# Four kinds of small products taken off TensorE, and the instruction order of a hybrid attention, DeltaNet and expert layer planned anew

## The chip, the cores and the metric

The kernel runs on one core of a Trainium2 chip. The metric is the device time of one execution in microseconds (us), from its first to its last instruction with what lies around it. Each time below is such a time, or a stretch of the one execution that the profiler recorded.

## What is computed

Two layers work on 256 latent tokens and 256 context tokens of width 1024. Each layer has a token mixer and a mixture of sixteen experts; the second layer needs results for the latent tokens alone.

```
for l in range(2):
    m_lat, m_ctx = six rows each of silu(c) @ mod_w[l] + mod_b[l]     # shift, scale, gate; twice
    h = modulate(x, ...)                                              # both streams
    q, k, v, qkv, z, a, b, gates = split(h @ w_in[l])                 # one projection
    A: differential attention, 2-D rotary positions on the latent q and k
       rope: x1*cos - x2*sin, x2*cos + x1*sin
    B: qkv = silu(short_conv(qkv)); q, k scaled to unit length over 128 channels
       g = cumsum of log decays; decay[i, j] = exp(g[i] - g[j]) where i >= j
       a_mat = beta * (k k^T) * decay (strict); solve (I + a_mat) against values
       out = q state + (q k^T * decay) v_new; the state goes on from chunk to chunk, both directions
    x = layer_norm(alpha*x + gate * (sig(gA)*(A @ w_pa) + sig(gB)*(B @ w_pb)) @ w_o)
    router: 4 groups of 4 experts, the best group, in it the best 2
    x = layer_norm(alpha*x + gate * sum of w * (silu(h@w1[e]) * (h@w3[e])) @ w2[e])
```

## The kernel before

**Strands.** The kernel is written as some ninety generators ("strands"): `modulation`, `conv_worker`, `norms`, `build`, `double`, `scan`, `att_worker`, `expert_up` and so on, one or several per stage and layer. A strand yields a class of buffer (`page`: 128x2048 words, twenty of them; `t5`: 128x512, sixteen; `tiny`; `bank`: the eight PSUM banks) or an `Event`, and records operations through helpers (`mm`, `tr`, `tt`, `stt`, `cpy`, `dma`). Since helpers record, the profile's lines are theirs: L451 is `mm`, L463 `mm_beside`, L468 `tr` (transpose on TensorE against the identity), L489 `tt`, L518 `stt`, L485 `cpy` on ScalarE, L537 `dma`.

**Planner.** While the program is being built, `Scheduler.run` keeps a clock of its own. Each helper gives its operation a duration (`dve`, `acte`, `n / 2400` for a fast product). `plan` estimates when a strand's first operation could begin; among those that could begin within 0.05 us of the earliest, the one whose strand has the lowest number in `PRIO` is emitted. So estimated durations and `PRIO` fix the order in every engine's queue, and each queue then runs in that order, whatever the real times are. That holds for SP's queue too, on which the weight loads and most other transfers stand: a transfer emitted behind a load that waits for its page waits with it.

**Stages.** Weights are loaded in 1 MB pieces in the order of `PLAN` (`loader`), split into a high and a low part for three fast products (`splitter`, `mm3`), and multiplied. In layer 0 projections, convolutions, the inverse of the decay matrix and attention run interleaved; then come the gates, the output projection, and the router (a run of small VectorE operations). Fourteen of the sixteen experts' weights can be asked for only when the router has ranked them (`pos_ev`). Layer 1 repeats this.

**Places that the change touches.**
- `modulation`: products of `csil` with `mod_w` leave four partial sums on the partitions; for eight of a layer's twelve pieces `mm(bk[:2, :], K["sel2"], part, True, True)` adds them with one float32 product of 512 columns (two TensorE records).
- `conv_worker`: `mm(Y.sqs[...], a4[:, t, :], ones[:, 0:1], True, True)` sums squares over channels, one product per head and tile of 128 tokens, into one PSUM bank (`sqb`) that stays taken through the stage, until `sq_end`.
- `build` and `double` call `grow`, which makes rows of cumulated decays with four transposes of a column spread over 128 columns, into a bank; `stt` reads them from there.
- `double` computes, per (tile, direction), part of the inverse (its products are 32 and 64 rows high) and, behind a wait for the q convolution, the matrix P = q k^T * decay.
- `att_worker`: the rotary swap of 16-row halves is `mm(b.v(256), K["perm"], lat, True, True)`, then three `tt`.

Of the kernel before, what the change touches and what calls it, by code (L numbers as in the profile page):

```python
# [38 lines left out]
def slot0(l, q):  # L39
# [15 lines left out]
PRIO = {"0ab": 2.106, "0att": 5.949, "0atte": 5.963, "0attend0": 3.942, "0attend1": 2.095, "0attw0": 3.982, "0attw1":  # L55
# [16 lines left out]

def const_layout():
# [5 lines left out]
    blk["perm"] = (r == (c ^ 16))  # L79
# [17 lines left out]
    blk["selR"] = (q[:, None] == np.arange(16)[None, :])  # L97
    blk["neg16"] = np.where(q < 16, -1.0, 0.0)[:, None]
# [52 lines left out]
class Op:  # L151
    __slots__ = ("opts", "outs", "ins", "ready", "nbytes", "pen", "rows")

    def __init__(self, opts, outs, ins, nbytes=0, pen=0.0):
        self.opts, self.outs, self.ins, self.nbytes, self.pen = opts, outs, ins, nbytes, pen
        self.ready = None
        self.rows = ins[-1].shape[0] / 128 if opts[0][0] == "PE" else 0.0
# [11 lines left out]
class Scheduler:  # L169
# [4 lines left out]
    PE_IN, PE_OUT = 0.1, 0.06  # L174
    DGE = 0.45
    TICK, COLUMNS = 10.24 / 3, 3060

    def __init__(self, make):
# [8 lines left out]
        self.now = 0.0  # L187
        self.columns, self.floor = {}, {}
# [142 lines left out]
    def plan(self, op):  # L331
# [15 lines left out]
    def emit(self, op, o, st):  # L347
# [5 lines left out]
        if eng == "PE":  # L353
            k = int(st / self.TICK)
            self.columns[k] = self.columns.get(k, 0.0) + op.opts[0][1] * 2400 * op.rows
            end += self.PE_OUT
        if op.nbytes:
# [6 lines left out]
            end = x + max(op.nbytes / 410e3, 0.1)  # L364
# [41 lines left out]
def tile_kernel(ctx, tc, x_in, c_in, ctx_in, cctx_in, mod_w, mod_b, w_in, conv_w, lam_q1, lam_k1, lam_q2,  # L406
# [13 lines left out]
    inv_dram = [dp.tile([128, 256], F32, name=f"inv{i}_dram") for i in range(2)]  # L420

# [37 lines left out]
    def mm_beside(os, as_, bs, start, stop):  # L459
# [4 lines left out]
        SC.rec([("PE", width(bs[0]) / 600 + 0.008 * len(os), f)], list(os), [*as_, *bs])  # L464

    def tr(o, a, idn=None):
        idn = ident if idn is None else idn
        SC.rec([("PE", 0.11, lambda: PE.transpose(o, a, idn))], [o], [a])  # L468
# [14 lines left out]
    def cpy(o, a):  # L483

        SC.rec([("ACT", acte(width(o), in_psum(a)), lambda: S.activation(o, a, AF.Copy, bias=0.0, scale=1.0)),  # L485
                ("DVE", dve(width(o), in_psum(a), 0.5), lambda: V.tensor_copy(o, a))], [o], [a], pen=1.0)
# [6 lines left out]
    def neg(o, a):  # L493
        SC.rec([("ACT", acte(width(o), in_psum(a)), lambda: S.activation(o, a, AF.Copy, bias=0.0, scale=-1.0)),
                ("DVE", dve(width(o), in_psum(a), 0.5), lambda: V.tensor_scalar(o, a, -1.0, None, op0=OP.mult))],
# [6 lines left out]
    def ts(o, a, s1, op0, s2=None, op1=None):  # L502
# [4 lines left out]
        SC.rec([("DVE", dve(width(o), in_psum(a), 0.5), f)], [o], aps(a, s1, s2))  # L507

    def affine(o, a, s, b):

        SC.rec([("ACT", acte(width(o), in_psum(a)), lambda: S.activation(o, a, AF.Identity, bias=b, scale=s)),
                ("DVE", dve(width(o), in_psum(a), 0.5),
# [8 lines left out]
    def vcopy(o, a):  # L521
        SC.rec([("DVE", dve(width(o), in_psum(a), 0.5), lambda: V.tensor_copy(o, a))], [o], [a])
# [2048 lines left out]
```

## Time and profile before

| | us |
|---|---|
| median of 3 runs | 1632.36 (1616.32 to 1634.97) |
| the profiled execution | 1628.14 |
| its span | 1626.0 |
| TensorE busy in it | 1493.8 |
| VectorE busy | 931.7 |
| ScalarE busy | 535.8 |

The span is the stretch from the first to the last instruction; 2.14 us of the profiled execution lie around it. PE is TensorE's products, PEld its weight loads, DVE VectorE, ACT ScalarE, POOL GpSimd, SP the queue of the sync engine. "Busy" of PE is the time covered by products, whose ends are modelled. PEclk is the granted share of TensorE's full clock of 2.4 GHz; 0.5 is the lower level, 1.2 GHz.

### The profile page before, as it was taken

The numbers are of one execution on the slowest core, as the hardware profiler recorded it, in microseconds if no ns is written. First come the engines' busy times: TensorE is split into PE (matmuls) and PEld (weight loads), VectorE is DVE, ScalarE is ACT, GpSimd is POOL, SyncE is SP. The second block draws the span as 40 slices with busy tenths as digits, with TensorE's granted clock in tenths as the row PEclk, the third lists the DMA queues.
The fourth block names the chain that finished last, engine by engine and source line by source line (L and its number), as shares of the span: only waits on it lengthen the run. The fifth ranks groups of instructions, "written<-read, shape, count | busy, mean of one in ns | idle before, by whom it ended". The sixth has DMA issues, their size and how long they took to land. (4 is left out here: it accounts for less than half of the span.)

```text
span 1626.0 us, 24829 instructions
## 1 busy us (share of the span) xinstructions
PE 1493.8 (92%) x9551; PEld 1017.6 (63%) x9552; DVE 931.7 (57%) x2391; ACT 535.8 (33%) x950; POOL 63.1 (4%) x84
## 2 busy tenths in 40 slices
PE   5999999999999977999999899999999957999974
PEld 2776788756787843465564367788889844454421
DVE  1677945768437586365575966792778666210023
ACT  2533343434331121264553253343554302110110
POOL 1000000000000001111010000000000000000000
PEclk9999999999999997999998999996999977999988
DMA  9415522152336577799998743440055955899994
GB/s 312 158 53 175 160 57 80 50 210 91 117 130 249 190 302 283 277 422 403 417 383 326 260 151 109 156 102 5 28 182 176 312 218 214 304 421 421 420 408 203
DMA packets 147725, 363.17 MB, mean 223 GB/s; under 512 B 27932, under 2 KB 82284, under 8 KB 122256
## 3 DMA queue, kind: packets, MB, share of 16 engines
q1 hardware_dynamic: 139808, 342.91, 56.9%
q0 software_dynamic: 6512, 16.38, 3.0%
q10 hardware_dynamic: 1280, 2.23, 0.4%
q8 instruction: 77, 1.26, 0.3%
q14 instruction: 48, 0.39, 0.1%
HBM read 345.47 MB, written 21.56 MB: 226 GB/s over the span
## 5 line engine op out<-in xcount | busy, mean ns | idle before, releaser
L451 PE MATMUL bank<-page,page 128*128 128x512 f32 (+3 forms) x3776 | 733.7, 349 | 13.5 <-ACT page L485 6.5
L451 PEld LDWEIGHTS bank<-page,page 128*128 128x128 f32 (+2 forms) x3776 | 567.6, 189 | 126.1 <-issue 27.3
L489 DVE TENSOR_TENSOR page<-page,page 128x1024 fp32r<-128x1024 f32 (+3 forms) x219 | 250.8, 1164 | 96.9 <-ACT page L485 94.9
L485 ACT ACTIVATE page<-page 128x1024 fp32r<-128x1024 f32 (+1 forms) x196 | 200.3, 1046 | 122.8 <-PE bank L451 65.8
L463 PE MATMUL bank<-page,t 128*64 128x512 f32 (+2 forms) x736 | 208.9, 607 | 6.8 <-DMA page<-in_w_exp_dram 5.9
L485 ACT ACTIVATE t<-bank 128x512 f32<-128x512 f32 (+5 forms) x168 | 79.8, 480 | 306.7 <-PE bank L468 210.5
L489 DVE TENSOR_TENSOR t<-bank,t 128x512 f32<-128x512 f32 (+3 forms) x63 | 49.6, 792 | 188.0 <-PE bank L463 153.8
L485 ACT ACTIVATE page<-bank 128x512 f32<-128x512 f32 (+2 forms) x127 | 70.2, 557 | 222.1 <-PE bank L451 97.9
L463 PE MATMUL bank<-page,page 128*32 128x512 f32 (+2 forms) x512 | 136.0, 604 | 8.0 <-DMA page<-in_w_exp_dram 7.6
L463 PEld LDWEIGHTS bank<-page,t 128*64 128x64 f32 (+2 forms) x736 | 64.6, 147 | 103.4 <-issue 87.1
L451 PE MATMUL bank<-t,page 32*32 32x16 f32 (+4 forms) x1472 | 117.1, 244 | 2.1 <-DVE t L504 1.8
L451 PEld LDWEIGHTS bank<-t,page 128*128 128x128 f32 (+3 forms) x1472 | 104.9, 160 | 18.9 <-issue 11.3
L468 PE MATMUL bank<-cf,t 128*128 128x128 f32 (+2 forms) x468 | 79.1, 287 | 36.0 <-DVE t L489 25.9
L468 PEld LDWEIGHTS bank<-cf,t 128*128 128x128 f32 (+2 forms) x468 | 54.8, 144 | 70.6 <-DVE t L489 31.8
L463 PEld LDWEIGHTS bank<-page,page 128*32 128x32 f32 (+2 forms) x512 | 47.0, 144 | 81.2 <-issue 67.1
L451 PE MATMUL bank<-page,csil 128*32 128x512 f32 x384 | 68.0, 678 | 17.2 <-DMA page<-in_mod_w_dram 16.5
L451 PE MATMUL bank<-page,t 128*128 128x512 f32 (+2 forms) x392 | 81.4, 346 | 2.1 <-DVE page L489 1.1
L451 PEld LDWEIGHTS bank<-page,t 128*128 128x128 f32 (+1 forms) x392 | 56.0, 185 | 26.4 <-issue 9.2
L518 DVE SCALAR_TENSOR_TENSOR t<-bank,tiny,t 128x508 f32<-128x508 f32 (+3 forms) x96 | 66.5, 700 | 7.5 <-ACT t L480 6.4
L480 ACT ACTIVATE t<-bank,tiny 128x512 f32<-128x512 f32 (+1 forms) x72 | 44.6, 623 | 53.5 <-PE bank L451 27.8
L480 ACT ACTIVATE page<-page 128x512 f32<-128x512 f32 (+2 forms) x44 | 25.6, 588 | 84.1 <-DVE page L489 48.5
L468 PE MATMUL bank<-cf,page 128*128 128x128 f32 (+1 forms) x248 | 41.7, 305 | 9.9 <-DMA page<-h_dram,cd 8.4
(178 smaller groups left out, 1139.7 us busy)
## 6 DMA issues: line engine op xcount, KB each, us to landing
page<-in_w_exp_dram SPq DMA_DIRECT2D x192, 1024.0 KB
page<-in_mod_w_dram SPq DMA_DIRECT2D x48, 1024.0 KB
page<-in_w_in_dram SPq DMA_DIRECT2D x44, 1024.0 KB
page<-in_w_o_dram SPq DMA_DIRECT2D x8, 1024.0 KB
y_dram<-t POOLq DMA_DIRECT2D x6, 1024.0 KB, 8.3
page<-m_dram SPq DMA_DIRECT2D x12, 512.0 KB
page<-y_dram SPq DMA_DIRECT2D x6, 1024.0 KB
page<-in_w_pb_dram SPq DMA_DIRECT2D x4, 1024.0 KB
```

The costliest lines, as they stand in the source:

```text
L451: lambda: PE.matmul(o, a, b, start=start, stop=stop, skip_group_check=True))], [o], [a, b])
L463: PE.matmul(o, a, b, start=start, stop=stop, skip_group_check=True)
L468: SC.rec([("PE", 0.11, lambda: PE.transpose(o, a, idn))], [o], [a])
L480: SC.rec([("ACT", acte(width(o), in_psum(a)), lambda: S.activation(o, a, f, bias=bias, scale=scale, **k))], aps(o, accum_out), aps(a, bias ...
L485: SC.rec([("ACT", acte(width(o), in_psum(a)), lambda: S.activation(o, a, AF.Copy, bias=0.0, scale=1.0)), ("DVE", dve(width(o), in_psum(a), ...
L489: opts = [("DVE", dve(width(o), in_psum(a) or in_psum(b)), lambda: V.tensor_tensor(out=o, in0=a, in1=b, op=op)), ("POOL", 0.1 + width(o) * ...
L518: lambda: V.scalar_tensor_tensor(o, a, s, b, op0=op0, op1=op1, **k))],
```

## The change

- `grow` is gone. `decay_gates` writes the cumulated decays of a layer once to a DRAM tensor (`gc_dram`, 16 KB); `build` reads them back spread over all partitions with one 1 MB transfer per pair of tiles, on SP; `double` asks for the rows again per (tile, direction), 256 KB each, on SP (`sum_rows`).
- The part of `double` behind the inverse becomes strands of its own (`decayed`).
- Squares are summed by four products side by side (32 columns each, on `ones`), a copy, and one short product per tile; no bank stays taken.
- The partial sums of the modulation rows are split into a high and a low part and added by two fast products with 16 columns.
- The rotary swap is a VectorE shuffle into a `t5`.
- The planner's durations are other ones, a change of product shape is charged 0.09 us (`TURN`), a transfer on the ACT queue 0.45 us, and all of `PRIO` is new.

```diff
-PRIO = {"0ab": 2.106, "0att": 5.949, ...
+PRIO = {"0ab": 2.106, "0att": 5.949, ...
...
+    TURN = 0.09
...
+                if op.kind != self.kind:
+                    o = (o[0], o[1] + self.TURN, o[2])
...
-            end = x + max(op.nbytes / 410e3, 0.1)
+            end = x + max(op.nbytes / 420e3, 0.1)
...
+    gc_dram = [dp.tile([32, 128], F32, name=f"gc{l}_dram") for l in range(2)]
...
-        t = n / 2400 if b.dtype == BF or (b.dtype == F32R and n >= 256) else n / 600
+        t = n / 2250 if b.dtype == BF or (b.dtype == F32R and n >= 256) else n / 600
...
-            t = max(t, width(a) / 1200)
+            t = max(t, width(a) / 580)
...
     def dve(n, ps, r=1.0):
-        return 0.065 + n * 0.00104 * (1.0 if ps else r) + (0.06 if ps else 0.0)
+        return 0.15 + n * 0.00104 * (1.0 if ps else r) + (0.02 if ps else 0.0)
     def acte(n, ps):
-        return (0.05 if ps else 0.093) + n * 0.000834
+        return (0.175 if ps else 0.21) + n * 0.00082
...
-        SC.rec([(q, 1.0 if q == "POOL" else 0.45 if q == "SP" else 0.1, lambda: eng.dma_start(o, a))], [o], [a],
+        SC.rec([(q, 1.0 if q == "POOL" else 0.45, lambda: eng.dma_start(o, a))], [o], [a],
...
-            cpy(part, bk)
+            if kind < 2:
+                cpy(part, bk)
+            else:
+                lo_ = yield "t5"
+                split(pt_.r(512), lo_.r(512), bk)
...
-                mm(bk[:2, :], K["sel2"], part, True, True)
-                tt(part[:2, :], bk[:2, :], br, OP.add)
+                mm(bk[:16, :], sel2r, pt_.r(512), True, False)
+                mm(bk[:16, :], sel2r, lo_.r(512), False, True)
+                tt(br, bk[:2, :], br, OP.add)
...
-        Y.sqb = yield "bank"
-        Y.sqs = Y.sqb.v(2, 4, 4)
+        Y.sq = {}
...
-                for t in range(2 * ns):
-                    mm(Y.sqs[:, 1 - part, 2 * s0 + t, hd:hd + 1], a4[:, t, :], ones[:, 0:1], True, True)
+                Y.sq[part, hd] = a_
...
+        b = yield "bank"
+        n0 = 256 if Y.last and part == 0 else 0
+        mm_beside([b.v(512)[32 * hd:32 * hd + 32, n0:] for hd in range(4)], [ones[:, :32]] * 4,
+                  [Y.sq[part, hd].v(512)[:, n0:] for hd in range(4)], True, True)
+        st = yield "t5"
+        cpy(st.v(512)[:, n0:], b.v(512)[:, n0:])
...
+        for t in range(n0 // 128, 4):
+            mm(b.v(4, 16)[:, t], st.v(4, 128)[:, t], K["selH"], True, True)
...
+        tr(b.v(128)[:32], gv[:, 6, :])
+        cpy(rows_.v(128)[:32], b.v(128)[:32])
+        dma(dram(gc_dram[l], 0, [[128, 32], [1, 128]]), rows_.v(128)[:32])
...
-    def grow(Y, b, t, d):
-        for hd in range(4):
-            tr(b.v(4, 128)[:, hd, :], hcol(Y.GC, t, d, hd).to_broadcast([128, 128]))
-        return b.v(4, 128)
+    def sum_rows(Y, t, d):
+        dma(cell(Y.pA, t, d).rearrange("p h j -> p (h j)"),
+            dram(gc_dram[Y.l], (t * 8 + d * 4) * 128, [[0, 128], [1, 512]]))
...
+        if t % 2 == 0:
+            dma(Y.pA[si].v(2048), dram(gc_dram[Y.l], si * 2048, [[0, 128], [1, 2048]]))
+            SC.set(Y.gc_ev[si])
+        yield Y.gc_ev[si]
...
             if t in Y.tiles:
-                for hd in range(4):
-                    yield Y.conv_ev[0, hd]
-                b = yield "bank"
-                gr = grow(Y, b, t, d)
...
+                sum_rows(Y, t, d)
+            else:
+                SC.set(Y.p_ev[t, d])
+            SC.set(Y.u_ev[t, d])
+
+    def decayed(Y, groups):
+        for t, d in groups:
+            if t not in Y.tiles:
+                continue
+            yield Y.u_ev[t, d]
+            for hd in range(4):
+                yield Y.conv_ev[0, hd]
+            A = cell(Y.pA, t, d)
...
-                b = yield "bank"
-                mm(b.v(256), K["perm"], lat, True, True)
-                tt(tmp.v(256), b.v(256), K["sin"], OP.mult)
-                SC.free(b)
-                tt(lat, lat, K["cos"], OP.mult)
-                tt(lat, lat, tmp.v(256), OP.add)
+                SC.rec([("DVE", dve(256, False), lambda o=tmp.v(256), a=lat:
+                         V.stream_shuffle(out=o, in_=a, mask=[c ^ 16 for c in range(32)]))], [tmp.v(256)], [lat])
+                tt(tmp.v(256), tmp.v(256), K["sin"], OP.mult)
+                tt(tmp.v(256, o=256), lat, K["cos"], OP.mult)
+                tt(lat, tmp.v(256, o=256), tmp.v(256), OP.add)
```

## Rows read from the trace of the kernel before

**Rows 1.** The page: busy us of each engine (share of the span), instructions.

```profile
PE 1493.8 (92%) x9551; PEld 1017.6 (63%) x9552; DVE 931.7 (57%) x2391; ACT 535.8 (33%) x950; POOL 63.1 (4%) x84
```

**Rows 2.** Windows: stretch, length, busy us of each engine (count), PEclk, DMA, GB/s.

```profile
50.00:200.00 150.00, 149.08 (x815) 112.30 (x814) 114.65 (x285) 56.13 (x88) 2.50 (x5) 1.00 0.40 120
200.00:300.00 100.00, 99.45 (x1365) 84.19 (x1365) 50.88 (x151) 40.40 (x106) 2.56 (x5) 1.00 0.21 65
300.00:600.00 300.00, 288.60 (x1644) 216.47 (x1643) 192.28 (x503) 94.72 (x179) 6.60 (x6) 0.99 0.48 168
600.00:680.00 80.00, 63.14 (x256) 29.89 (x258) 41.59 (x182) 13.44 (x22) 9.56 (x9) 0.85 0.76 285
680.00:870.00 190.00, 181.07 (x845) 111.34 (x843) 114.99 (x179) 101.13 (x127) 20.45 (x22) 0.97 0.96 385
870.00:950.00 80.00, 71.16 (x291) 30.57 (x288) 58.33 (x109) 25.60 (x42) 0.00 (x0) 0.92 0.76 287
950.00:1050.00 100.00, 98.05 (x562) 73.29 (x560) 66.28 (x152) 37.17 (x60) 0.99 (x2) 0.98 0.44 139
1050.00:1200.00 150.00, 149.14 (x1640) 126.77 (x1639) 100.40 (x301) 65.86 (x156) 4.09 (x8) 0.90 0.20 53
1200.00:1300.00 100.00, 96.50 (x772) 89.82 (x771) 73.67 (x180) 46.15 (x75) 1.64 (x2) 1.00 0.74 252
...
1400.00:1626.00 226.00, 195.96 (x878) 81.08 (x876) 39.57 (x77) 27.06 (x48) 6.98 (x7) 0.96 0.89 368
```

**Rows 3.** The chain that ended last, near its end: start us, us, what.

```profile
1584.92 19.70 DMA page<-in_w_exp_dram
```

**Rows 4.** PE by line and shape: out<-in, rows*columns, moved shape, xcount | busy, mean ns.

```profile
L468 PE MATMUL bank<-cf,t 128*128 128x128 f32 x456 | 77.2, 288 | 29.6 <-DVE t L489 25.9 <-DVE t L518 2.0 <-DVE tiny L518 1.2
...
L451 PE MATMUL bank<-t,cf 128*2 128x512 f32 x32 | 16.3, 592 | 2.4 <-ACT t L485 2.4
...
L451 PE MATMUL bank<-page,page 128*16 128x512 f32 x48 | 14.3, 439 | 2.0 <-ACT page L485 1.3 <-DVE page L489 0.7
...
L451 PE MATMUL bank<-ones,t 128*128 128x1 f32 x112 | 13.8, 242 | 0.2 <-ACT t L480 0.2
...
L451 PE MATMUL bank<-page,cf 128*128 128x256 f32 x32 | 10.2, 399 | 0.0
```

**Rows 5.** PE's timeline at five places: start us, us, instructions merged (xcount).

```profile
60.67 0.95 PE L451 MATMUL bank<-ones,t 128*128 128x1 f32 x8
...
112.99 0.62 PE L451 MATMUL bank<-page,cf 128*128 128x256 f32 x2
113.45 0.95 PE L468 MATMUL bank<-cf,t 128*128 128x128 f32 x8
114.32 0.96 PE L451 MATMUL bank<-page,page 128*128 128x512 f32 x3
...
196.56 1.02 PE L451 MATMUL bank<-t,cf 128*2 128x512 f32 x2
197.51 0.44 PE L451 MATMUL bank<-t,t 32*32 32x16 f32 x32
...
204.09 1.06 PE L451 MATMUL bank<-page,csil 128*32 128x512 f32 x8
```

**Rows 6.** DVE and ACT by line and shape, columns as in the group by shape above.

```profile
L489 DVE TENSOR_TENSOR page<-page,bank 128x512 f32<-128x512 f32 x50 | 34.0, 684 | 27.2 <-PE bank L451 19.4 <-PE bank L468 7.3
...
L489 DVE TENSOR_TENSOR t<-bank,cf 128x256 f32<-128x256 f32 x16 | 6.7, 419 | 12.2 <-PE bank L451 12.2
...
L485 ACT ACTIVATE page<-bank 128x512 f32<-128x512 f32 x92 | 54.3, 595 | 153.7 <-PE bank L463 73.0 <-PE bank L451 58.7 <-PE bank L468 21.6
```

**Rows 7.** Windows again: layer 1's inverse, and its router.

```profile
1107.00:1140.00 33.00, 33.00 (x393) 29.74 (x392) 9.07 (x28) 9.52 (x28) 1.05 (x2) 0.67 0.01 1
1300.00:1360.00 60.00, 31.31 (x227) 27.18 (x227) 42.56 (x133) 6.29 (x13) 0.00 (x0) 0.67 0.40 160
```

**Rows 8.** Waits of SP's queue: who waited for whom, us in total, times, longest.

```profile
SPq L537 <- PE bank L451: 492.9, 60, 49.4
```

More of the change, by code (lines that the diff above doesn't have):

```diff
@@ L156, in __init__ @@
         self.ready = None
-        self.rows = ins[-1].shape[0] / 128 if opts[0][0] == "PE" else 0.0
+        pe = opts[0][0] == "PE"
+        self.rows = ins[-1].shape[0] / 128 if pe else 0.0
+        self.kind = (ins[0].shape[0], width(ins[0]) if len(ins) > 1 else 128, len(ins) > 2) if pe else None
 class Strand:
@@ L485, in cpy @@
         SC.rec([("ACT", acte(width(o), in_psum(a)), lambda: S.activation(o, a, AF.Copy, bias=0.0, scale=1.0)),
[L486 removed]
+                ("DVE", dve(width(o), in_psum(a), 0.62), lambda: V.tensor_copy(o, a))], [o], [a], pen=1.0)
     def tt(o, a, b, op, e="DVE"):
@@ L521, in vcopy @@
     def vcopy(o, a):
-        SC.rec([("DVE", dve(width(o), in_psum(a), 0.5), lambda: V.tensor_copy(o, a))], [o], [a])
+        SC.rec([("DVE", dve(width(o), in_psum(a), 0.62), lambda: V.tensor_copy(o, a))], [o], [a])
     def vset(o, x, e="DVE"):
@@ L839, in modulation @@
                 bk = b.v(512)
-                mm(bk[:2, :], K["sel2"], part, True, True)
-                tt(part[:2, :], bk[:2, :], br, OP.add)
-                dma(m_dram[l, :, i * 512:(i + 1) * 512], part[:2, :], "ACT")
+                mm(bk[:16, :], sel2r, pt_.r(512), True, False)
+                mm(bk[:16, :], sel2r, lo_.r(512), False, True)
+                tt(br, bk[:2, :], br, OP.add)
+                SC.free(lo_)
+                dma(m_dram[l, :, i * 512:(i + 1) * 512], br, "ACT")
                 SC.free(br_)
@@ L1052, in norms @@
             yield Y.conv_ev[part, hd]
-        w, w2 = yield ("tiny", "tiny")
-        o = 8 if Y.last and part == 0 else 0
+        b = yield "bank"
[4 more added lines that the diff above has]
+        cpy(st.v(512)[:, n0:], b.v(512)[:, n0:])
+        SC.free(b, *(Y.sq.pop((part, hd)) for hd in range(4)))
+        w, w2, b = yield ("tiny", "tiny", "bank")
+        o = n0 // 32
         sq, z = w.v(16)[:, o:], w2.v(16)[:, o:]
-        vcopy(sq, Y.sqs[:, 1 - part].rearrange("p a b -> p (a b)")[:, o:])
+        for t in range(n0 // 128, 4):
+            mm(b.v(4, 16)[:, t], st.v(4, 128)[:, t], K["selH"], True, True)
+        vcopy(shaped(sq, (4 - n0 // 128, 4)), b.v(4, 16)[:, n0 // 128:, :4])
+        SC.free(b, st)
         rsqrt(Y.gv[:, 13 - part, o:16], sq, 1.0, z)
@@ L1139, in decay_gates @@
         SC.free(b)
+        b, rows_ = yield ("bank", "t5")
+        tr(b.v(128)[:32], gv[:, 6, :])
+        cpy(rows_.v(128)[:32], b.v(128)[:32])
+        dma(dram(gc_dram[l], 0, [[128, 32], [1, 128]]), rows_.v(128)[:32])
+        SC.free(b, rows_)
         act(EGC, GC, AF.Exp)
@@ L1313, in double @@
             SC.free(b, wt)
-            SC.set(Y.u_ev[t, d])
             Y.di_left[si] -= 1
@@ L1318, in double @@
             if t in Y.tiles:
-                for hd in range(4):
-                    yield Y.conv_ev[0, hd]
-                b = yield "bank"
-                gr = grow(Y, b, t, d)
-                for hd in range(4):
-                    stt(A[:, hd], gr[:, hd], hcol(Y.GC, t, d, hd), capP[:, d], OP.subtract, OP.min)
-                SC.free(b)
-                act(A, A, AF.Exp)
-                b = yield "bank"
-                for hd in range(4):
-                    mm(b.v(4, 128)[:, hd], Y.kq(hd)[:, t, 0, :], Y.kq(hd)[:, t, 1, :], True, True)
-                tt(A, A, b.v(4, 128), OP.mult)
-                SC.free(b)
+                sum_rows(Y, t, d)
[10 more added lines that the diff above has]
+            A = cell(Y.pA, t, d)
+            for hd in range(4):
+                stt(A[:, hd], A[:, hd], hcol(Y.GC, t, d, hd), capP[:, d], OP.subtract, OP.min)
+            act(A, A, AF.Exp)
+            b = yield "bank"
+            for hd in range(4):
+                mm(b.v(4, 128)[:, hd], Y.kq(hd)[:, t, 0, :], Y.kq(hd)[:, t, 1, :], True, True)
+            tt(A, A, b.v(4, 128), OP.mult)
+            SC.free(b)
             SC.set(Y.p_ev[t, d])
@@ L2433, in open_layer @@
         Y.pu_ev = [Event(f"pu{i}") for i in R2]
+        Y.gc_ev = [Event(f"gc{i}") for i in R2]
         Y.blk_ev = [Event(f"blk{i}") for i in R4]
@@ L2484, in open_layer @@
             sp(double(Y, [(a + 1, 1), (a, 1)]), 2.76 + .02 * si, f"dbl{si}b")
+            for n, o in enumerate(([(a, 0), (a + 1, 0)], [(a + 1, 1), (a, 1)])):
+                sp(decayed(Y, o), 1.8, f"dec{si}{'fb'[n]}")
         for d in R2:
@@ L2530, in tile_kernel @@
     SC.spawn(loader(), 0, "loader")
-    SC.spawn(splitter(), 1, "splitter")
-    SC.spawn(modulation(0), 1.5, "mods")
-    SC.spawn(modulation(1), 6.2, "mods1")
+    SC.spawn(splitter(), PRIO.get("splitter", 1), "splitter")
+    SC.spawn(modulation(0), PRIO.get("mods", 1.5), "mods")
+    SC.spawn(modulation(1), PRIO.get("mods1", 6.2), "mods1")
     SC.spawn(load_x(A), 0, "x")
@@ L2537, in tile_kernel @@
     B.prev = A
-    SC.spawn(vectors(B), 8, "vec")
+    SC.spawn(vectors(B), PRIO.get("1vec", 8), "vec")
     SC.run(ex)
```

36 lines of the change are left out of this document (17 added, 19 removed), and 33 rows, old and new, of the table PRIO.

## The prediction

> **What bounds the kernel now.** The page's first part comes first: TensorE's products cover 92% of the span, VectorE 57%, ScalarE 33% [rows 1]. Such a mean mixes stages, so the windows by stage come next [rows 2]. The reader is to see two kinds of stretch. From 50 to 300 us and from 950 to 1300 us products cover 96 to 99% of the time while the DMA share is mostly 0.20 to 0.48: there TensorE sets the pace. From 680 to 870 us and from 1400 us on, the DMA share is 0.96 and 0.89 at 385 and 368 GB/s: there the experts' weights set it, and the chain of waits agrees, since near its end it stands 19.7 us on one expert load [rows 3]. These loads can only be asked for once the router has ranked the experts. So the span is a TensorE-bound way to router 0, a DMA-bound stretch, a TensorE-bound way to router 1, and a DMA-bound stretch. What is saved ahead of a router moves all that follows forward; what is saved behind it stays there. All four kinds of product that go stand ahead of a router, nearly all in the covered stretches.
>
> Within those stretches one loss stands out: in layer 1's inverse the granted clock was 0.67 over 33 us (some at 2.4, some at 1.2 GHz), though products covered all of it; what ran were mostly products of 32 and 64 rows and short ones [rows 7]. That cost 33 x (1 - 0.67) = 10.9 us. In layer 0 the same work, from 200 to 300 us, kept a clock of 1.00 between broad projections [rows 2].
>
> **The products that go.** Here the pitch counts, not the mean duration, since one product's end overlaps the next one's beginning.
>
> Transposes of `grow`: `build` has 8 groups of four per layer, `double` 8 in layer 0 and 4 in layer 1, 28 groups, 112 transposes. Eight of them start at 113.45 and the next product at 114.32 us [rows 5]: 0.109 us each, 12.2 us in all. From the other side, busy time over count is 77.2 / 456 = 0.169 us [rows 4], 19.0 us. I take 12.2, because the next product does begin then.
>
> Sums of squares: 112 records cover 13.8 us [rows 4]. In come four sums side by side, one of half width; eight such records take 1.06 us in `modulation`'s products with `csil` [rows 5], so 3.5 x 1.06 = 3.7 us; and 14 short products of two records at 0.95 / 8 = 0.119 us as the old ones had [rows 5], 3.3 us. Net 6.8 us.
>
> Rotary swap: 16 products of two records. One starts at 112.99 and its successor at 113.45 us [rows 5]: 0.46 us, 7.4 in all; by the busy time 10.2 [rows 4]. I take 7.4.
>
> Modulation rows: 16 products of two records at 0.95 us (196.56 to 197.51) [rows 5], 15.2 us, by the busy time 16.3 [rows 4]. In come 32 fast records with 16 columns; the trace's nearest cover 14.3 us for 48, 0.30 us each [rows 4], 9.5 us. Net 5.7, at most 6.8.
>
> Sum: 12.2 + 6.8 + 7.4 + 5.7 = 32.1 us, at most 42.8; at least nothing, if products are not what the stage waits for (a rival below). I take 32.
>
> The Trainium skill ("Trainium Kernel Development and Optimization", section Performance Expectations) warns that the time covered by matmuls is a bad measure, because they are pipelined, and names the share of weight loads instead. Here that is 63% against 92% [rows 1]; by it a third of TensorE's time is slack, and the sum would be nearer to half of 32 than to all. The high cover with hardly a wait in it makes me keep 32, and the warning as a rival.
>
> **What comes in elsewhere.** VectorE gets 16 shuffles of 256 columns, not in the trace; the nearest row is an operation on two inputs of that size, 0.42 us [rows 6], so between nothing and 6.7 us; I take 6.7. It gets 16 subtractions of 512 columns from PSUM, 0.684 us each [rows 6], 10.9 us. Together 17.6 us. VectorE was idle for 35 of 150 us, 49 of 100, 34 of 100 and 50 of 150 in the four stretches concerned [rows 2], so I cost it at nothing; without that cover it would be up to 17.6 us.
>
> The rows of decays come back as four transfers of 1 MB and twelve of 256 KB, 7 MB; at the 385 GB/s of the full stretch [rows 2] 19 us of transfer, in stretches where the engines for DMA were at 0.20 to 0.44. Nothing, unless they come late. They stand on SP's queue, whose longest wait for a page was 49.4 us [rows 8]; behind a late row wait `build` and the inverse, or `decayed` and then `scan`. This is the rival on the other side.
>
> The split of `double` frees the second group of each strand from the q convolution, and no bank is held for the sums. Both take away waits, but PE hardly waits there, so nothing.
>
> **The order.** All queues are ordered anew, and no row can price that. What rows can tell is whether the new durations are nearer to the chip. A ScalarE copy of 512 columns from PSUM took 0.595 us [rows 6]; the old formula gives 0.477, the new one 0.595. A VectorE operation of that size took 0.684 [rows 6]; old 0.657, new 0.702. So a planned time is nearer to the real one. What could an order win? At most the 10.9 us of lowered clock, and the uncovered time of three stretches: 11.4 (300 to 600), 16.9 (600 to 680) and 8.8 us (870 to 950) [rows 2], 48 us in all. The router's stretch of 1300 to 1360 us, with 28.7 us uncovered [rows 7], is a run of dependent VectorE operations that no order shortens. What could it lose? If layer 0's small products came to stand by themselves, 100 us at 0.67 would cost 33 us. Between a gain of 48 and a loss of 33 I take a gain of 15: the lowered clock, and a tenth of the uncovered time.
>
> **The sum.** Span 1626 - 32 - 15 = 1579; with the 2.14 us around it the execution would take 1581. The runs' median stands 1632.36 / 1628.14 = 1.0026 above the profiled execution, so 1585 us, 2.9% less. A measurement of this kernel tells about 2% from no change, as its three runs spread over 1.1%: under 1600 counts as faster, over 1665 as slower.
>
> **Rivals.**
> 1. *Time handed back.* In inverse and scan, chains of short products go through VectorE and ScalarE; with transposes gone, their successors wait for those. Half of 32 is left and the order wins nothing: span 1610, 1616 us. For it: the share of weight loads, and VectorE's 115 of 150 us in the first stretch [rows 2]. Against: only 0.9 of 150 us were uncovered there [rows 2].
> 2. *The clock.* With fewer broad operations between them, the small products of 200 to 300 us get the clock of layer 1: 1626 - 32 + 33 = 1627, so 1633 us. For it: the 33 us [rows 7]. Against: projections remain to be mixed in. The Trainium skill ("TensorE: Matmul & The Clock Gate", section HAM oscillation) has the clock fall when TensorE pauses; the stretch at 0.67 was covered all through, so the trace does not agree that pauses are needed. By that rule this rival would not come about at all.
> 3. *Slower: rows of decays late on SP.* If in each layer one fetch stood behind a page wait of 49.4 us [rows 8] with scan behind it, 1579 + 98.8 = 1678, so 1684 us. It decides from 40 us per layer on. For it: such waits exist, and `scan` needs P for each step. Against: `decayed` has no need of its rows until the inverse and the q convolution are done, and the planner places fetches by when pages come free.
> 4. *The order wins all it can*: 1626 - 32 - 48 = 1546, so 1552 us.
>
> **Chances.** Forecast 0.50, its own range 1562 to 1606, a tenth of it over 1600; rival 1 0.20 (1606 to 1632); rival 2 0.07; rival 3 0.10; rival 4 0.13 (1540 to 1562). Faster: 0.45 + 0.13 = 0.58. Within 2%: 0.05 + 0.20 + 0.07 = 0.32. Slower: 0.10. The range of 1548 to 1640 leaves out rival 3 and the lower half of rival 4.
>
> **What would show it.** The groups by shape should lack `ones` with one column and `page,cf` with 256, and have 112 transposes fewer; busy time of PE should fall by about 32 us, and the uncovered time from 50 to 300 us not rise. Router 1's ranking, and with it the last loads, should come about 47 us earlier, while the stretch from there to the end keeps its length. Rival 1 shows as PE waits for DVE or ACT in the covered stretches, rival 2 as PEclk under 1.00 in layer 0's inverse, rival 3 as PE, DVE and SP waits for transfers from `gc_dram`. I am wrong if the stretch behind a router changes by more than 15 us, for then the DMA-bound stages are not the fixed part I take them for.

## The result and the profile after

The changed kernel took 1664.33 us (median of 4 runs, 1659.06 to 1674.33), the kernel before beside it 1625.32 (4 runs). The ratio is 1.0257, with a 95% interval of 1.0207 to 1.0306: slower, where 1585 was forecast, and outside the range of 1548 to 1640. The profiled execution took 1660.55 us, its span is 1658.8.

Where did 32.8 us of span (1658.8 - 1626.0) come from? The operation on VectorE that writes `Mb`, by which the experts are ranked, marks the two routers. Its row in the view of that tile, for before and after (count, shortest/median/longest in ns, first and last start in us):

```profile
L489 DVE TENSOR_TENSOR Mb<-t x2: 191/208/224, 608.4 to 1352.5; 128x64 bf16<-128x64 f32 x1, 128x32 bf16<-128x32 f32 x1
```
```profile
L499 DVE TENSOR_TENSOR Mb<-t x2: 191/208/224, 640.3 to 1377.1; 128x64 bf16<-128x64 f32 x1, 128x32 bf16<-128x32 f32 x1
```

Router 0 is 31.9 us later. From router 0 to router 1 the kernel needs 736.8 us and not 744.1, and behind router 1 281.7 and not 273.5; these two nearly cancel. So nearly the whole loss lies ahead of router 0. The windows of that stretch and of layer 1 up to its router (from about layer 1's first transposes on), before and then after (stretch, length, busy us of PE, PEld, DVE, ACT and POOL with counts, granted clock, DMA share, GB/s):

```profile
0.00:608.40 608.40, 569.34 (x3983) 430.55 (x3984) 376.03 (x1003) 208.81 (x405) 19.36 (x34) 0.99 0.46 155
928.50:1352.50 424.00, 388.39 (x3264) 325.20 (x3263) 290.75 (x749) 169.94 (x332) 6.71 (x12) 0.91 0.43 141
```
```profile
0.00:640.40 640.40, 575.15 (x3872) 433.04 (x3873) 389.56 (x1040) 207.31 (x397) 19.57 (x34) 0.92 0.46 154
955.00:1377.00 422.00, 377.96 (x3201) 313.16 (x3200) 299.06 (x783) 167.24 (x329) 6.69 (x12) 0.92 0.44 149
```

There are 111 products fewer on the way to router 0, and yet they cover 5.8 us more, and 65.3 us are uncovered, that is, without a product running (640.4 - 575.15), where it was 39.1. The trace also lists when which of the two levels of the clock was granted. Laid over that list, 75.9 of the 575 covered us ran at the lower level (before: 4.5). If a microsecond there counts as half a one, 38.0 us were lost to it, against 2.3. That closes the account: work at full clock 567.1 to 537.2, so 29.9 less; 26.2 more uncovered; 35.7 more lost to the clock; together +32. Of the last two, 48.5 us lie between 50 and 300 us. The 29.9 can't be held against the forecast's 32, which were for both layers, and it is good to some 8 us only: the same 3872 products, in the order of `after_searched` below, come to 545.6 and not 537.2.

The stages that answer to [rows 2], and three places within them:

```profile
50.00:200.00 150.00, 129.67 (x784) 91.63 (x782) 101.34 (x281) 48.97 (x86) 2.44 (x5) 0.88 0.35 107
200.00:300.00 100.00, 94.97 (x919) 74.35 (x920) 54.92 (x134) 36.32 (x79) 2.56 (x5) 0.87 0.26 85
300.00:600.00 300.00, 289.34 (x1785) 230.58 (x1785) 189.38 (x496) 99.70 (x192) 3.05 (x4) 0.98 0.45 154
...
140.00:160.00 20.00, 8.24 (x48) 5.03 (x46) 19.48 (x81) 5.28 (x9) 0.99 (x2) 0.77 0.24 48
...
153.00:157.00 4.00, 0.83 (x2) 0.20 (x2) 3.85 (x18) 1.11 (x2) 0.15 (x1) 0.50 0.23 44
...
190.00:235.00 45.00, 40.32 (x431) 28.94 (x430) 12.35 (x25) 16.61 (x44) 0.53 (x1) 0.73 0.30 93
```

From 50 to 300 us, where TensorE had been covered but for 1.5 us at a clock of 1.00 [rows 2], 25.4 us are uncovered and the clock is 0.88 and 0.87. The worst place is 140 to 160 us: TensorE works for 8.24 us, VectorE for 19.48. In the kernel before, TensorE covered all 20 of them:

```profile
140.00:160.00 20.00, 20.00 (x104) 11.83 (x104) 16.52 (x50) 8.37 (x12) 0.00 (x0) 1.00 0.73 223
```

The timeline of the changed kernel there, in cuts (start us, us, engine, line, merged instructions, idle time before and its releaser):

```profile
146.00 2.15 DVE L528 SCALAR_TENSOR_TENSOR page<-bank,t,page 128x128 f32<-128x128 f32 x8
...
149.99 2.15 DVE L528 SCALAR_TENSOR_TENSOR page<-bank,t,page 128x128 f32<-128x128 f32 x8
152.05 1.13 DVE L528 SCALAR_TENSOR_TENSOR page<-page,t,cb 128x128 f32<-128x128 f32 x4
...
153.22 0.63 ACT L490 ACTIVATE page<-page 128x512 f32<-128x512 f32 x1 [2.83 <-DVE page L528]
...
153.75 0.58 ACT L495 ACTIVATE t<-bank 128x512 fp32r<-128x512 f32 x1
...
154.38 0.61 PE L461 MATMUL bank<-t,sel2t 128*16 128x512 f32 x1 [7.36 <-ACT t L495]
...
156.41 0.45 SPq L547 DMA_DIRECT2D page<-in_w_in_dram  x1
...
156.78 0.61 PE L461 MATMUL bank<-t,sel2t 128*16 128x512 f32 x1 [1.79 <-DVE t L499]
...
162.02 1.06 ACT L495 ACTIVATE page<-page 128x1024 fp32r<-128x1024 f32 x1 [7.69 <-DMA page<-in_w_in_dram]
...
163.13 2.05 PE L461 MATMUL bank<-page,page 128*128 128x512 f32 x3 [5.74 <-ACT page L495]
```

Read the first pause from its end, at 154.38 us. The new product for the modulation rows (`sel2t`) waits 7.36 us for ScalarE's rounding copy (L495); that copy stands on ScalarE behind `build`'s exponentials (L490), and these wait for `build`'s `stt` on VectorE, which follow each other almost without a break. The reading from here on is argued, and no run tests it by itself: before, each group of `build` had four transposes on TensorE to wait for, so TensorE paced it; now VectorE does, and the next product on TensorE's queue that needs either engine waits.

The pause of 5.74 us behind it ends otherwise, though its row names ScalarE too: that copy splits a piece of weights and had itself waited 7.69 us for the load, which SyncE's queue issued only at 156.41 us, behind stores of the inverse that wait for the same `stt`.

The granted clock is 0.50, which is 1.2 GHz, from 151.0 to 168.0 us, and again from 185.1 to 209.0 and from 229.5 to 236.3 us, where many small products of the inverse run (0.73 in the mean from 190 to 235 us). It fell inside the pause of 7.36 us, at the end of one of 2.46 (from 182.72 us) and just behind one of 2.68 (from 225.80 us).

The Trainium skill ("TensorE: Matmul & The Clock Gate", section HAM oscillation) has the clock fall when TensorE pauses; the trace agrees at these three places. In layer 1's inverse before [rows 7] it does not: there the clock was lower from 1098.0 to 1128.8 us, with no pause of half a microsecond from 1000 to 1200 us.

### The profile page after: what moved, and what is told of

The parts are those of the page before. It is cut to its first block, busy times and chain, and to the rows that moved or that the text cites. A ratio compares the mean times of both kernels' runs of the same rounds, so it can differ in the third digit from the quotient of the medians.

```text
span 1658.8 us, 24553 instructions
## 1 busy us (share of the span) xinstructions
PE 1487.4 (90%) x9357; PEld 1006.1 (61%) x9358; DVE 954.7 (58%) x2459; ACT 533.2 (32%) x939; POOL 63.6 (4%) x84
## 5 line engine op out<-in xcount | busy, mean ns | idle before, releaser
L461 PE MATMUL bank<-page,page 128*128 128x512 f32 (+3 forms) x3776 | 735.2, 352 | 24.6 <-ACT page L495 13.4
L461 PEld LDWEIGHTS bank<-page,page 128*128 128x128 f32 (+2 forms) x3776 | 574.8, 192 | 146.4 <-issue 27.3
L499 DVE TENSOR_TENSOR page<-page,page 128x1024 fp32r<-128x1024 f32 (+4 forms) x219 | 250.4, 1163 | 103.4 <-ACT page L495 101.6
L495 ACT ACTIVATE page<-page 128x1024 fp32r<-128x1024 f32 (+1 forms) x193 | 197.3, 1046 | 146.4 <-PE bank L461 81.1
L473 PE MATMUL bank<-page,t 128*64 128x512 f32 (+2 forms) x736 | 217.9, 628 | 10.2 <-DMA page<-in_w_exp_dram 9.9
L495 ACT ACTIVATE t<-bank 128x512 f32<-128x512 f32 (+6 forms) x172 | 81.2, 478 | 362.1 <-PE bank L478 244.1
L499 DVE TENSOR_TENSOR t<-bank,t 128x512 f32<-128x512 f32 (+3 forms) x79 | 60.5, 769 | 201.6 <-PE bank L473 108.4
L495 ACT ACTIVATE page<-bank 128x512 f32<-128x512 f32 (+2 forms) x125 | 68.7, 554 | 192.4 <-PE bank L461 85.3
L461 PEld LDWEIGHTS bank<-t,page 32*32 32x32 f32 (+3 forms) x1472 | 106.6, 161 | 19.5 <-issue 7.7
L461 PE MATMUL bank<-page,csil 128*32 128x512 f32 x384 | 74.1, 708 | 26.5 <-DMA page<-in_mod_w_dram 25.8
L478 PE MATMUL bank<-cf,t 128*128 128x128 f32 (+2 forms) x358 | 62.9, 293 | 26.3 <-DVE t L499 14.3
L461 PE MATMUL bank<-page,t 128*128 128x512 f32 (+2 forms) x392 | 76.8, 340 | 1.6 <-DVE page L528 1.4
L478 PEld LDWEIGHTS bank<-cf,t 128*128 128x128 f32 (+2 forms) x358 | 43.0, 147 | 55.6 <-issue 33.6
L490 ACT ACTIVATE t<-bank,tiny 128x512 f32<-128x512 f32 (+1 forms) x72 | 44.6, 622 | 52.8 <-DVE tiny L514 30.0
```

Source lines behind the costliest of these rows:

```text
L461: lambda: PE.matmul(o, a, b, start=start, stop=stop, skip_group_check=True))], [o], [a, b])
L473: PE.matmul(o, a, b, start=start, stop=stop, skip_group_check=True)
L478: SC.rec([("PE", 0.112, lambda: PE.transpose(o, a, idn))], [o], [a])
L499: opts = [("DVE", dve(width(o), in_psum(a) or in_psum(b)), lambda: V.tensor_tensor(out=o, in0=a, in1=b, op=op)), ("POOL", 0.1 + width(o) * ...
```

## Experiments

Each is timed beside the kernel before on one chip; its ratio to that is given with its 95% interval. A plan's end is the planner's own clock when the last operation is emitted; the distance is the chip's time less that.

### The products by themselves

`dbl_products`: the kernel before in its order, the four kinds of product issued twice.

```diff
-        mm(b.v(256), K["perm"], lat, True, True)
+        mm(b.v(256), K["perm"], lat, True, True, times=2)   # so too the transposes of grow, ones, sel2
```

> The kernel before with its order untouched; each of the four kinds of product is issued twice (112 transposes of decays, 56 sums of squares, 16 rotary swaps, 16 sums of modulation rows), which changes no result. By their pitch that is 12.2 + 13.8 + 7.4 + 15.2 = 48.6 us more work for TensorE. Theory A (TensorE sets the pace ahead of the routers, the products are worth their pitch, and the new order is what cost time): 40 to 50 us slower than the kernel before. Theory B (products were hidden in waits, their pitch is not what the stage waits for): under 25 us slower.

1671.26 us, 1.0291 (1.0234 to 1.0349): 46.3 us more, of the 48.6 that their pitch (start to start) adds up to, and within theory A's 40 to 50. So the pitch was the right price of one more product in these covered stretches. That one less gives as much back is not shown by it.

### Products and order apart

`products_old_plan`: the changed kernel with the old durations and, for the strands that existed, the old priorities. `old_products_new_plan`: the kernel before with the new durations, turns and priorities, and the changed kernel's wait for `code_ev`. `old_plan_jitter`: the kernel before, each priority changed by up to 1%.

```diff
-    TURN = 0.09
+    TURN = 0.0                 # products_old_plan; so too n / 2250 -> n / 2400, dve, acte as before
-PRIO = {... new ...}
+PRIO = {... that of before ...}
```

> The changed kernel's products, with the durations and priorities of the kernel before (no charge for a change of shape; the new strands have their default priority). Theory A (order costs, products gain): faster than the kernel before by 15 to 35 us. Theory B (the replacements cost more than the products): slower than before by 20 to 45 us, like the changed kernel.

1643.58 us, 1.0124 (1.0073 to 1.0174): 19 us slower, where theory A expected 15 to 35 less; it lies just under the 20 to 45 of theory B. Its trace has the same pause as the changed kernel, ended by the same copy:

```profile
144.30 0.61 PE L460 MATMUL bank<-t,sel2t 128*16 128x512 f32 x1 [7.30 <-ACT t L494]
```

> The kernel before's products, with the changed kernel's durations and priorities (and its one added wait of a scatter for its codes, without which the new order is not sound). Theory A: slower than the kernel before by 45 to 80 us, since it has the new order and none of the savings. Theory B: within 15 us of the kernel before.

1719.58 us, 1.0569 (1.0504 to 1.0634): the new order alone costs 95 us on the old products, more than the 45 to 80 expected. Its windows from 50 to 300 us:

```profile
50.00:200.00 150.00, 135.60 (x754) 97.93 (x752) 105.53 (x281) 50.28 (x79) 2.50 (x5) 0.96 0.33 104
200.00:300.00 100.00, 94.93 (x844) 75.11 (x845) 40.70 (x93) 32.55 (x72) 2.04 (x4) 0.87 0.28 87
```

So 19.5 us are uncovered there with the transposes still in place. The product for the modulation rows waits for its copy behind `build` here too, at 155.29 us, but 3.28 us and not 7.36. In this pair the products' going made the pause longer, and under the old order it made it (none before, 7.30 in `products_old_plan`).

> The kernel before with every priority multiplied by a random factor between 0.99 and 1.01; durations and products as before. It measures what an order that nobody aimed at costs. Theory A with an order that matters much: 5 to 30 us slower than before. Theory B with an order that matters little: within 5 us.

1630.95 us, 1.0044 (1.0004 to 1.0085): one random change of 1% costs the old priorities 6 us.

### Durations and priorities apart; SP's queue

> The changed kernel with its own priorities, but with the old formulas for the durations and no price for a turn of the array. Theory 'the order is a search that ended worse' says that the planner's own end of its plan, plus an offset that belongs to its set of durations, tells the chip's time: with the old durations the chip was 128 us over the plan for the kernel before (1625 over 1497) and 123 over it for the run with the products alone (1644 over 1521); this plan ends at 1509, so 1632 to 1637 us, about 30 less than the changed kernel. Theory 'priorities belong to the durations that they were chosen under': a mix of old durations and new priorities is slower than the changed kernel, 1675 to 1720. Theory 'the new durations themselves are at fault': 1590 to 1625, as the products' 32 to 48 us come through.

1637.37 us, 1.0068 (1.0027 to 1.0110), as the search theory said (1632 to 1637): 27 us less than the changed kernel. That priorities belong to the durations they were chosen under (1675 to 1720) is refuted.

> The changed kernel with its own durations, but with the priorities of the kernel before for all strands that it has. Search theory: with the new durations the chip was 29 us over the plan (1664 over 1634) and 28 over it in the run with the old products (1720 over 1692); this plan ends at 1680, so 1708 to 1710 us. Theory 'priorities belong to their durations': slower than the changed kernel too, 1675 to 1720, which does not tell it from the first. Theory 'the new durations are at fault, not the priorities': within 15 of the changed kernel, 1650 to 1680.

1682.83 us, 1.0372 (1.0302 to 1.0442). The search theory's 1709 misses; that the durations alone do it (1650 to 1680) is missed by 3; the theory refuted above would have had 1675 to 1720.

> The kernel before with its own products and priorities, but with the new durations and the price for turns. Search theory: plan 1697 plus 28, so 1725 us. Priorities belong to their durations: slower than before by 40 to 100, 1665 to 1725. Durations at fault: about as slow as the run with both (1720). If the durations did no harm by themselves and the new priorities did it all, it would stay within 15 of the kernel before, 1610 to 1640.

1685.54 us, 1.0405 (1.0338 to 1.0472): 62 us for the durations, with old products and old priorities (the run also has the changed kernel's wait for `code_ev`, which is not priced by itself). The search theory's 1725 misses here too, so with the new durations the distance from plan to chip isn't fixed.

`after_pool_queue` keeps the order and moves the issue of three kinds of transfer.

```diff
-        dma(N, blk_dram[si], "SP")
+        dma(N, blk_dram[si], "SP", by="POOL")     # planned as SP's, issued by GpSimd
```

> The changed kernel in its own order, with the small transfers of the inverse (blocks out to DRAM and back, and the inverses back) issued from GpSimd's queue and no longer from SyncE's, where they stand behind stores that wait for VectorE. Theory 'the pauses of TensorE in layer 0 come from what stands behind these stores on SyncE's queue': 15 to 40 us less than the changed kernel, and TensorE's waits between 150 and 240 us mostly gone. Theory 'VectorE paces build once the transposes are gone': TensorE still waits at 140 to 160 us and the time stays within 8 us of the changed kernel.

1673.46 us, 1.0330 (1.0265 to 1.0395), 9 more than the changed kernel; "within 8" is missed by 1, and the two intervals overlap. The first pause is the same (timeline of TensorE, then the window):

```profile
153.45 0.61 PE L461 MATMUL bank<-t,sel2t 128*16 128x512 f32 x1 [7.36 <-ACT t L495]
...
140.00:160.00 20.00, 8.15 (x43) 4.67 (x41) 17.20 (x72) 5.66 (x10) 9.53 (x17) 0.78 0.31 73
```

What stood on SyncE's queue behind the stores is therefore not the cause of the first pause, though SyncE did wait there (waits of its queue in the changed kernel: total us, times, longest):

```profile
SPq L547 <- DVE page L528: 70.9, 9, 29.4
...
SPq L547 <- ACT t L490: 36.7, 2, 27.6
```

It did end the second pause: here the load that was issued at 156.41 us stands at 128.10 us, and that wait is gone. But nothing is won, since TensorE now waits 4.30 and 3.39 us for VectorE in its place (to 158.35 and to 163.20 us), and 25.9 us are uncovered from 50 to 300 us where it was 25.4.

### Is the order bad, or only unfinished?

`after_searched`: the changed kernel's products, the old durations, and new priorities. They were found by changing a few at random and keeping what ended the plan earlier. `before_searched` is the control, the kernel before treated likewise. `after_jitter` changes the changed kernel's priorities by up to 1%. `after_old_pe_prices` takes back TensorE's rates and `TURN` alone.

```diff
-PRIO = {"0ab": 2.106, "0att": 5.949, ...}
+PRIO = {... the numbers of the plan that ended first ...}
```

> The changed kernel's products with the old durations, and priorities found by some 2,500 plans (a few numbers changed at random, kept when the planner's own end was earlier, now and then when it was a little later), begun from the changed kernel's priorities. The plan ends at 1470 us, 39 before that of the run with the old durations alone. Theory 'the products are worth their pitch, and the chip follows the old durations' plan at a fixed distance': the distance was 127, 123, 128 and 128 us in four kernels (1624 over 1497, 1644 over 1521, 1637 over 1509, 1631 over 1503), so 1470 + 127 = 1597, 1590 to 1605. Theory 'without the transposes VectorE and the lowered clock take back whatever the products give': the planner does not see that, and the time stays at 1625 to 1645.

1596.24 us, 0.9853 (0.9785 to 0.9922): 1597 was expected.

> The kernel before, products and durations, with priorities searched in the same way from its own; control for the run above. The plan ends at 1487 us, 10 before that of the kernel before. At the fixed distance of 127: 1614, 1608 to 1620, so that of the 27 us between the kernel before and the searched changed kernel 10 belong to the search and 17 to the products. If the kernel before had the best order that its products allow on the chip, not only in the plan: 1624 or above.

1608.71 us, 0.9927 (0.9891 to 0.9964), a little better than the 1614 expected (1608 to 1620). The windows of the searched changed kernel, and under them of the searched kernel before:

```profile
50.00:200.00 150.00, 146.85 (x895) 109.08 (x894) 121.90 (x314) 61.66 (x104) 2.51 (x5) 1.00 0.46 141
200.00:300.00 100.00, 99.79 (x1303) 84.94 (x1303) 58.55 (x167) 44.82 (x110) 2.50 (x5) 1.00 0.24 75
...
0.00:596.10 596.10, 551.05 (x3872) 415.74 (x3873) 384.14 (x1031) 210.32 (x406) 19.31 (x34) 0.98 0.50 166
915.50:1325.50 410.00, 374.53 (x3186) 314.14 (x3185) 298.21 (x771) 166.71 (x329) 6.67 (x12) 0.91 0.46 154
```
```profile
0.00:605.80 605.80, 565.89 (x3983) 429.64 (x3984) 378.99 (x1005) 209.22 (x403) 19.36 (x34) 0.98 0.46 157
921.00:1330.80 409.80, 383.74 (x3264) 320.19 (x3263) 291.25 (x746) 171.72 (x335) 6.72 (x12) 0.94 0.43 146
```

With the same products as the changed kernel, 50 to 300 us is covered again but for 3.4 us, at a clock of 1.00, and router 0 comes at 596.1 us. So these products do not need the pauses and the low clock; an order can avoid them. Between the two searched kernels the products give 12.5 us by the medians. In the two profiled executions router 0 is 9.7 us earlier (596.1 against 605.8), and in layer 1 nothing is left: 410.0 against 409.8 us. There the work at full clock is 20.3 us less, as counted above, but 9.4 more are uncovered and 11.1 more lost to the clock. This holds for one execution each: when the searched changed kernel was profiled again (`searched_once_more`), 720.0 us lay between its routers and not 729.4, where the searched kernel before has 725.0.

> The changed kernel with each priority changed by up to 1% at random, everything else kept; the same change cost the kernel before 6 us. Theory 'the new order is a narrow hit in a rough landscape': the plan ends at 1677 us, 43 later than unchanged, and with the new durations the chip stood from 12 below to 30 above the plan, so 1665 to 1707. Theory 'the new order is slow for what its products and queues do, whatever the priorities': within 10 of the changed kernel, 1654 to 1674.

1699.65 us, 1.0507 (1.0434 to 1.0580), in the 1665 to 1707 expected of a narrow hit: 35 us for a change of 1% that cost the old order 6. Each is one random draw, and the plan's own end had moved with it, by 43 and by 6 us.

> The changed kernel with its priorities and its new durations for VectorE, ScalarE and the transfers, but with TensorE's old rates and no price for a turn. If the dearer products and turns are what leads the planner astray: 1630 to 1645, as with all the old durations (1637). If the durations of VectorE and ScalarE are: 1655 to 1675, as in the changed kernel. The plan ends at 1602.

1679.66 us, 1.0379 (1.0310 to 1.0449), slower than either guess: with TensorE's old prices alone the plan ended 32 us earlier and the chip 15 later. The other half, old durations for VectorE and ScalarE with TensorE's new prices, was not run, so no group of durations is shown to be the culprit, and none is cleared.

> The changed kernel, products and new durations as they are, with priorities searched further from its own by some 5,000 plans in the same way; the plan ends at 1604 us, 30 before that of the changed kernel. Theory 'only the search under the new durations was unfinished': as far below the changed kernel as the plan, 1664 - 30 = 1634 (with the distances of minus 12 to plus 30 seen so far, 1592 to 1634). Theory 'plans made with the new durations are worse on the chip as such, and a better plan by them is no better kernel': 1650 to 1680.

1635.68 us, 1.0104 (1.0039 to 1.0169). The plan ended 30 us earlier and the kernel is 29 us faster than the changed one, as the theory of the unfinished search had it (1634). So part of the loss was an unfinished search. It still is 39 us behind `after_searched`, found with about half as many plans.

### VectorE's new work

`searched_vector_twice`, and again side by side with the searched kernel in five rounds (`searched_once_more`, `vector_twice_once_more`); the order is kept.

```diff
-                split(pt_.r(512), lo_.r(512), bk)
+                split(pt_.r(512), lo_.r(512), bk, times=2)   # the subtraction; so too stream_shuffle
```

> The searched kernel in its order, with VectorE's new work issued twice: the 16 stream shuffles (0.438 us each in the changed kernel's trace) and the 16 subtractions of 512 columns for the modulation rows (0.684), 7.0 + 10.9 = 17.9 us more on VectorE, nothing more elsewhere. If VectorE's work is covered by TensorE, as the prediction had it: within 3 of the searched kernel, 1593 to 1600. If it stands on the path now that the products are gone: 6 to 18 more, 1602 to 1614.

1609.25 us, 0.9938 (0.9902 to 0.9973); the searched kernel had 1596.24 on another chip.

> The searched kernel again, as the other half of the next run's comparison, on the same chip and in the same rounds: 1596 us as before, ratio to the kernel before 0.980 to 0.990.

> The searched kernel with VectorE's new work issued twice, again. The first time its median was 13 us above the searched kernel's, while the profiled executions stood 1.7 us the other way. If VectorE's 17.9 us are covered: within 3 us of the searched kernel beside it. If they stand on the path: 6 to 18 above it.

1593.57 us, 0.9851 (0.9802 to 0.9900), and 1603.96, 0.9929 (0.9894 to 0.9964): 10.4 us for VectorE's second helping. That is within the 6 to 18 of "on the path", though the ends of the two intervals just overlap. The shuffles' rows, once and twice:

```profile
L1563 DVE STREAM_SHUFFLE t<-page 128x256 f32<-128x256 f32 x16 | 7.0, 439 | 0.0
```
```profile
L1564 DVE STREAM_SHUFFLE t<-page 128x256 f32<-128x256 f32 x32 | 14.1, 441 | 0.0
```

All orders in one table, times in us, ordered by the plan's set of durations:

| kernel | products | durations | priorities | plan's end | chip | chip - plan |
|---|---|---|---|---|---|---|
| before | old | old | old | 1497 | 1625 | 128 |
| old_plan_jitter | old | old | old, 1% | 1503 | 1631 | 128 |
| products_old_plan | new | old | old | 1521 | 1644 | 123 |
| after_old_durations | new | old | new | 1509 | 1637 | 128 |
| before_searched | old | old | searched | 1487 | 1609 | 122 |
| after_searched | new | old | searched | 1470 | 1596 | 126 |
| after | new | new | new | 1634 | 1664 | 30 |
| after_jitter | new | new | new, 1% | 1677 | 1700 | 23 |
| after_old_priorities | new | new | old | 1680 | 1683 | 3 |
| old_products_new_plan | old | new | new | 1692 | 1720 | 28 |
| before_new_durations | old | new | old | 1697 | 1686 | -11 |
| searched_new_durations | new | new | searched | 1604 | 1636 | 32 |
| after_old_pe_prices | new | TensorE's old, others new | new | 1602 | 1680 | 78 |

The new durations put the plan's end some three quarters nearer to the chip (30 us of 128), and each of the four orders made with them that has a partner with the old ones is slower than it: by 62 (before), 39 (products_old_plan), 27 (after_old_durations) and 39 us (after_searched). The durations also decide whether ScalarE or VectorE makes a copy, but few move: 882 activations on ScalarE in the changed kernel, 893 in the searched one.

## Why the prediction was wrong

- **What bounds the kernel** held. The stretch from router 0 to layer 1 shrank by 5.5 us (314.6 against 320.1), that behind router 1 grew by 8.2; neither reached the 15 us set as the limit. Of the other signs, 112 transposes went, as said; but the uncovered time from 50 to 300 us rose from 1.5 to 25.4, and router 1 came 24.6 us later and not 47 earlier.
- **The products' term** held: work at full clock ahead of router 0 fell by 29.9 us, in layer 1 up to router 1 by 8.0 (362.8 to 354.8), 38 together against 32 taken and 42.8 at most. The two searched kernels agree: 13.2 (558.8 to 545.6) and 20.3 (366.9 to 346.6), 33.5 together. Doubling the old products cost 46.3 of 48.6. By group, against [rows 4], transposes fell from 77.2 to 60.4 us and the modulation rows from 16.3 to 12.5:

```profile
L478 PE MATMUL bank<-cf,t 128*128 128x128 f32 x344 | 60.4, 295 | 20.1 <-DVE t L499 14.3 <-DVE t L528 3.2 <-DVE tiny L499 1.1
...
L461 PE MATMUL bank<-t,sel2t 128*16 128x512 f32 x32 | 12.5, 433 | 10.2 <-ACT t L495 8.1 <-DVE t L499 2.1
```

  PE's busy time fell by 6.4 us only (1493.8 to 1487.4), since more of the products ran at the lower clock, where they are longer: the busy time that I had named as the sign of this step doesn't show it.
- **VectorE at nothing** failed. The prices were right (the shuffle 0.438 us, estimated at 0.42; VectorE's busy time rose by 23.0 us in all, against 17.6), the cover was not. I had read "idle for 35 of 150 us" [rows 2] as cover. A mean over 150 us says nothing of the 20 us in which VectorE works for 19.48. In the searched kernel 17.9 us more on VectorE cost 10.4. The dearest part may not even be among the additions: `build`, freed from its transposes, seems to run as fast as VectorE lets it. That is read from the timeline; no run puts the transposes alone back.
- **The rows of decays at nothing** held. All waits for them in the changed kernel, VectorE's and SyncE's:

```profile
DVE page L528 <- DMA page<-gc_dram: 0.5, 1, 0.5
...
SPq L547 <- DMA gc_dram<-t: 2.1, 2, 1.1
```

- **The order, -15 us, is the step that failed**, in sign and in its bound of +33. Alone, on the old products, it cost 95; on the new ones it is 68 behind the best order that was found with the old durations (1664 against 1596). The inference was "a planned time is nearer to the real one, so the order is better". Its first half is true (the distance fell from 128 to 30 us), its second does not follow. The plan's end ranks orders only under one set of durations, and it placed six of them at 122 to 128 us from the chip under the old set. Under the new set the orders found are worse, and, by one draw each, narrower (1% costs 35 us). The bound of 33 counted the lowered clock alone; that an order could also uncover TensorE had no price in it. Why a nearer estimate leads to worse orders stays open. By 300 us 1841 products have run in the changed kernel, 2323 before and 2333 in the searched one; but that may only be the loss seen from another side.
- **Rivals.** The first (VectorE and ScalarE hold TensorE up) and the second (layer 0's small products get the lowered clock) both came about, and together: 26 and 36 us on the way to router 0, where I had 16 and 33. I had priced them as alternatives. In this trace three of the five lowered stretches from 50 to 300 us begin in or just behind a pause of over 2 us, so they belong in one rival with one price; with the measured 26 and 36 that is 1585 + 62 + the 15 not won = 1662, which adds up what was measured and is no forecast. The third (rows late on SyncE) did not come about, but its mechanism did, on another transfer: a weight load stood on SyncE's queue and ended the pause of 5.74 us. PE's waits of 50 to 300 us in the changed kernel name VectorE, ScalarE and the modulation weights, and the second row's longest is that load:

```profile
PE bank L461 <- ACT t L495: 8.8, 5, 7.4
PE bank L461 <- ACT page L495: 7.2, 4, 5.7
PE bank L461 <- DMA page<-in_mod_w_dram: 3.4, 2, 2.7
...
PE bank L461 <- DVE t L499: 2.1, 2, 1.8
```

- **What the products give at best** was overstated even so. Between the two searched kernels it is 12.5 us and not 32. Some 10 of the difference are VectorE's added work, if the price of the second helping is that of the first; for the rest, layer 1's uncovered time and clock in the profiled execution are a candidate, but two executions of that kernel differ by 9.4 us there. As the two searches are two draws, the 12.5 has the luck of both in it.

## What to carry to other kernels

Work taken from the engine that sets the pace is worth its pitch only until another engine sets it, and where that happens must be read from windows of the length of one stage (20 us here), not from the idle share of 150. An order that is planned from estimates has to be priced as a draw: change its numbers by 1% first, more than once (one draw cost 6 us for the old, 35 for the new), and compare plans only under one set of estimates; that these estimates are nearer to the chip says nothing of the order. The best kernel here, 1.5% faster than before, keeps the new products, goes back to the old durations and searches the priorities anew.

## What the runs showed of the hardware

In a pause of 7.36 us the granted clock went to 0.50, and it came back at 168.0 us. From 185.1 us on, the end of another pause, it was 0.50 for 24 us, of which products covered 22.6; by count most of them have 32 rows. In the searched kernel, where no pause of 0.8 us lies between 86 and 300 us, 200 to 300 us has 1.00 with 1303 products. A stream shuffle of 128x256 words took 0.438 us, about what an operation on two inputs takes (0.415). Issuing the inverse's small transfers from GpSimd's queue in place of SyncE's brought no gain (1673 against 1664 us, with overlapping intervals): a weight load behind them was issued 28 us earlier, and TensorE waited for VectorE in its place.
